# The first phase's shift columns and first scale column: made by TensorE from chunks with the condition's features on the partitions, instead of by VectorE and GpSimd

## The chip, the cores and the metric

One Trainium2 chip, of which the kernel uses one core. The metric is the time of one execution on the device, in microseconds. TensorE makes the matrix products and accumulates them in PSUM; VectorE, ScalarE and GpSimd work elementwise; SyncE issues the transfers (DMA) from the chip's memory to SBUF. Each engine takes its own instructions in the order in which the program gives them, and waits on semaphores for the others.

## The reference

A trunk of two layers on 512 positions of width 1024, in float32. Every sub-layer normalises its input and modulates it by a shift, a scale and a gate that come from one conditioning vector `c` (of 1024 features) through a matrix `ada_w`:

```python
c_act = jax.nn.silu(c)
for l in range(DEPTH):
    mod = (c_act @ ada_w[l] + ada_b[l]).reshape(b, N_MOD, 1, D_MODEL)
    sh1, sc1, g1 = mod[:, 0], mod[:, 1], mod[:, 2]
    ...
    h = modulate(rmsnorm(x, norm_ffn1[l]), sh1, sc1)      # h * (1 + sc1) + sh1
    x = x + 0.5 * g1 * swiglu(h, ffn1_wi[l], ffn1_wo[l])  # silu(h @ gate) * (h @ up) @ wo
    h = modulate(rmsnorm(x, norm_mix[l]), sh2, sc2)
    x = x + g2 * token_mixing(h, ...)
    h = modulate(rmsnorm(x, norm_ffn2[l]), sh3, sc3)
    x = x + 0.5 * g3 * swiglu(h, ffn2_wi[l], ffn2_wo[l])
return rmsnorm(x, final_norm)
```

This case is about `sh1` and `sc1` of the first layer: nothing of the first feed-forward can be multiplied before they are there.

## The kernel before

**Tiling.** Activations lie with their 1024 features in eight chunks of 128 partitions and the 512 positions in the free dimension. A modulation vector (shift, scale or gate) is therefore eight *columns*, 128x1 each, chunk k on the 128 partitions. Column (l, ch, k) of layer l is kept in `mod[:, l, ch, k]`; ch 0 is `sh1`, ch 1 is `sc1`. With its bias and, for a scale, the gain of the norm it goes to `fin`.

**Products in three parts.** Every float32 operand is split into `hi` (rounded to the fp32r type, ScalarE) and `lo` (the rest, VectorE); `mm3` (L224 to L228) makes hi x hi, lo x hi and hi x lo into one PSUM tile, each a 128x128 by 128x512 product.

**The first phase.** The first 60 us or so make the first five weight chunks (five PSUM tiles `ps`, in `start`) in eight steps k = 0 to 7, one for each chunk of features. A step is 15 products: three for each of the five chunks. It needs

- the chunk's slices of weights, loaded for two steps at once as 128x256 pieces (`raw`, L988), with `hi` (L989) and `lo` (L991);
- the normalised input of chunk k (`make`): `t` = x times scale column times the norm's factor (VectorE, L296), `hh` = t + shift column rounded (ScalarE, L298), `hl` = the rest (VectorE, L299);
- so the scale column and the shift column of chunk k, in `fin` (ScalarE, L983 and L984).

**How a column is made.** `ada_w` is stored transposed, so a transfer of 512 KB (`araw`, 128 outputs on the partitions, 1024 features along the row, L310) is multiplied by silu(c), copied to all partitions, and summed along the row. VectorE does both in one instruction (L320). For the shift columns of steps 1, 3, 4, 6 and 7 (`BY_POOL`) GpSimd multiplies (L317) and ScalarE sums in a pass over the product (L318). silu(c) is there twice, in SBUF (`cs`) and in PSUM (`pc`, two banks); in this phase VectorE reads the one in PSUM. Four `araw` buffers go round: the transfer for a column is issued when the column two steps back is done.

**Ahead of the first step.** TensorE copies c to all partitions (L363), runs small products on the identity matrix (`warm`, L942), sums the squares over the features (`pstat`, L273: a 128x128 block against one column of ones) and, when VectorE has the norm's factor, spreads it over the partitions (`pR`, L284).

**What sets the order.** A scheduler orders each engine's instructions by the order of the program, raised by `high_priority` and held back by `issue_after`. Behind the phase TensorE goes on with the remaining weight chunks of the same feed-forward, while VectorE makes the other modulation columns between its own work.

Of the kernel before, what the change touches and what calls it, by code (L numbers as in the profile page):

```python
# [11 lines left out]
F32 = mybir.dt.float32  # L12
F32R = mybir.dt.float32r
I32 = mybir.dt.int32
AF = mybir.ActivationFunctionType
ALU = mybir.AluOpType
PSUM = bass.MemoryType.PSUM

L = 2
KD = 8  # L20
S = 512
# [35 lines left out]
HL = 200  # L57
BY_POOL = (1, 3, 4, 6, 7)
AW = 1.5
# [8 lines left out]
@with_exitstack  # L68
def tile_trunk(ctx: ExitStack, tc: tile.TileContext, xT, c, positions, adaT, cols, sink, wi1, wo1,
               wqk, wv, w_out, wi2, wo2, masks, freqs, out):  # L70
    nc = tc.nc
    V, A, T, G = nc.vector, nc.scalar, nc.tensor, nc.gpsimd

    const = ctx.enter_context(tc.tile_pool(name="const", bufs=1))
# [6 lines left out]
    early = ctx.enter_context(ExitStack())  # L81
    pc = early.enter_context(tc.tile_pool(name="pc", bufs=1, space=PSUM)).tile([128, 1024], F32, name="pc")
    pq = None


    home = ctx.enter_context(tc.tile_pool(name="home", bufs=1))
    V.memset(home.tile([128, 56], F32, name="pad"), 0.0)

    x = const.tile([128, KD, S], F32, name="x")
    col = const.tile([128, cols.shape[1]], F32, name="col")  # L90
    ident = const.tile([128, 128], F32, name="ident")
    ones = const.tile([128, 1], F32, name="ones")
    orow = const.tile([1, 128], F32, name="orow")
    V.memset(ones, 1.0)
    V.memset(orow, 1.0)
    mod = const.tile([128, L, 9, KD], F32, name="mod")
# [4 lines left out]
    snk = const.tile([128, L * 8], F32, name="snk")  # L101
    nsnk = const.tile([128, L * 8], F32, name="nsnk")


# [201 lines left out]
    def ada_raw(l, ch, k):  # L306
        home, tags = ada["pool"]
        tags.append(tags.pop(0))
        raw = home.tile([128, 1024], F32, tag=tags[0], name="araw")
        nc.sync.dma_start(raw, adaT[l, ch * KD + k])  # L310
        return raw

    def ada_col(l, ch, k, pool=False, raw=None, by=cs):
        if raw is None:
            raw = ada_raw(l, ch, k)
        if pool:
            G.tensor_tensor(raw, raw, cs, op=ALU.mult)  # L317
            A.activation(raw, raw, AF.Copy, accum_out=mod[:, l, ch, k:k + 1])  # L318
            return
        return V.tensor_tensor_reduce(out=raw, in0=raw, in1=by, scale=1.0, scalar=0.0, op0=ALU.mult,  # L320
                               op1=ALU.add, accum_out=mod[:, l, ch, k:k + 1]).ins
# [36 lines left out]

    def ada_load(pool):
        cr = pool.tile([1, 1024], F32, tag="raw2", name="cr")  # L360
        nc.sync.dma_start(cr, c)
        for j in range(2):
            T.matmul(pc[:, j * S:(j + 1) * S], orow, cr[:, j * S:(j + 1) * S], start=True, stop=True)  # L363

    def ada_open(pool):
        ada["pool"] = pool, ["araw", "araw1", "araw2", "araw3"]
        for dst in (cs, pc):
            for j in range(2):
                A.activation(dst[:, j * S:(j + 1) * S], pc[:, j * S:(j + 1) * S], AF.Silu)

# [562 lines left out]
    with tc.high_priority():  # L933
        A.activation(snk[0:1, 0:1], orow[0:1, 0:1], AF.Silu)
    ada_load(pool)
    make_identity(nc, ident)
# [7 lines left out]
    norm = Norm()  # L944
# [5 lines left out]
    warm(WARM[0])  # L950
    with tc.issue_after(norm.last):
        ada_open(pool)
    nc.sync.dma_start(col, cols)
    cg = pool.tile([128, S], F32, tag="raw5", name="cg")[:, :KD]
    V.scalar_tensor_tensor(cg, col[:, KD:2 * KD], 1.0, col[:, C_NF1:C_NF1 + KD], op0=ALU.add, op1=ALU.mult)
    sc0 = ada_col(0, 1, 0, by=pc)
    with tc.high_priority():
        with tc.issue_after(sc0):
            norm.stat(0, 4)
        warm(WARM[1])  # L960
        norm.bcast(0, 4)
        warm(WARM[2])

    def start():
# [10 lines left out]
        norm.alloc()  # L975
        for k in range(KD):
            if k:
                with tc.issue_after(norm.first):
                    ada_col(0, 1, k, by=pc)
            with tc.issue_after(norm.first if k else norm.root):  # L980
                ada_col(0, 0, k, k in BY_POOL, by=pc)
            g = col[:, C_NF1 + k:C_NF1 + k + 1]
            A.activation(fin[:, 0, 1, k:k + 1], mod[:, 0, 1, k:k + 1], AF.Identity, scale=g, bias=cg[:, k:k + 1])  # L983
            A.activation(fin[:, 0, 0, k:k + 1], mod[:, 0, 0, k:k + 1], AF.Identity, bias=col[:, k:k + 1])  # L984
            if k % 2 == 0:
                ks = slice(k * 128, k * 128 + 256)
                for j, (raw, hi, lo) in enumerate(Ws):
                    nc.sync.dma_start(raw[:, ks], specs[j][:, ks])  # L988
                    A.activation(hi[:, ks], raw[:, ks], AF.Copy)  # L989
                    with nullcontext() if k else tc.issue_after(norm.root):  # L990
                        V.tensor_tensor(lo[:, ks], raw[:, ks], hi.bitcast(F32)[:, ks], op=ALU.subtract)  # L991
            with tc.high_priority():
                norm.make(k, 0, fin[:, 0, 1], fin[:, 0, 0], FULL)
            for (raw, hi, lo), p in zip(Ws, ps):
                mm3(p, (hi, lo), k, norm.h[k], FULL, k == 0, k == KD - 1)
# [183 lines left out]
```

## Time and profile before

| | us |
|---|---|
| median of 3 runs | 1952.32 (1952.02 to 1953.6) |
| the profiled execution | 1953.16 |
| its span, first to last instruction | 1951.4 |
| TensorE busy | 1907.5, 98% of the span |
| VectorE busy | 1514.6, 78% |
| ScalarE busy | 940.9, 48% |
| GpSimd busy | 84.7, 4% |

How to read the views: PE is TensorE's products, PEld its loads of weights, DVE is VectorE, ACT ScalarE, POOL GpSimd. PEclk is the share of full clock (2.4 GHz) that TensorE was granted in a stretch; 0.50 is its lower level, 1.2 GHz. In the windows each row is one stretch in us from the span's start, then its length, the busy time of each engine with its instructions, PEclk, the DMA share and GB/s. In the groups by line, behind the bar stand the busy us, the mean ns of one, and the idle us of the engine just before them with what ended them. In a timeline each row has start, us, engine, line, operation, out<-in, and in brackets the idle time before it. A float32 product of TensorE (`pstat`, `warm`, `pR`, `pc`) is shown as several passes with a weight load each; a product of `mm3` is one pass. The ends of passes are modelled and overlap the next start.

### The profile page before, as it was taken

The page shows a single profiled execution, that of the slowest core. Times are in us where ns is not written, and L with a number is a line of the kernel's source. Part 1 is how long each engine was busy: PE and PEld are TensorE (multiplying, and loading weights), DVE is VectorE, ACT ScalarE, POOL GpSimd, SP SyncE. Part 2 cuts the span into 40 slices and gives each one's busy share as a digit, 9 for nine tenths or more (in the row PEclk, how much of TensorE's full clock was granted, in tenths as well). Part 3 has the DMA queues.
Part 4 walks back from the last instruction along what each step waited for, and adds up shares of the span by engine and source line. Part 5 has one row for each costly group of instructions (what it writes and reads, how often), then busy time and mean ns, then how long its engine had stood idle before and what let it go on. Part 6 is the DMA issues. An engine that isn't in the chain of part 4 may idle for free.

```text
span 1951.4 us, 30979 instructions
## 1 busy us (share of the span) xinstructions
PE 1907.5 (98%) x12000; PEld 1714.8 (88%) x12000; DVE 1514.6 (78%) x2653; ACT 940.9 (48%) x1782; POOL 84.7 (4%) x63
## 2 busy tenths in 40 slices
PE   7999999999989999999999999999998999999998
PEld 5788888898777999989999898999887889898998
DVE  7967484477887989899688898867778889686773
ACT  5422222245674554536455363544566656353552
POOL 2000000021210000000000000000212000000000
PEclk8999999999999999999999999999999999999999
DMA  8878484244421246463424544342543113233231
GB/s 291 284 258 308 127 302 134 79 128 140 116 58 54 74 159 200 141 209 128 141 66 152 195 144 161 107 134 87 154 115 96 46 33 112 94 106 122 83 113 44
DMA packets 84677, 267.95 MB, mean 137 GB/s; under 512 B 10673, under 2 KB 13361, under 8 KB 84530
## 3 DMA queue, kind: packets, MB, share of 16 engines
q1 hardware_dynamic: 84530, 265.98, 42.4%
q8 instruction: 94, 1.54, 0.3%
q14 instruction: 53, 0.43, 0.1%
HBM read 244.97 MB, written 2.10 MB: 127 GB/s over the span
## 4 chain that ended last, share of the span: by engine, by line
PE 88%; DVE 5%; ACT 3%; issue 2%; DMA 2%; POOL 0%; SPq 0%; DVEq 0%; ACTq 0%; POOLq 0%
PE mm L226 17%; PE mm L227 17%; PE mm L228 16%; PE mm L488 10%; PE mm L489 9%; PE mm L490 9%; PE ptr L732 2%; PE po L739 1%; PE po L740 1%; PE s L698 1%; PE s L699 1%; DMA araw<-in_adaT_dram 1%; PE mm L661 1%; PE mm L662 1%; PE mm L663 1%
## 5 line engine op out<-in xcount | busy, mean ns | idle before, releaser
L157 ACT ACTIVATE hi<-raw 128x512 fp32r<-128x512 f32 (+5 forms) x253 | 215.2, 865 | 301.3 <-PE mm L228 213.7
L158 DVE TENSOR_TENSOR lo<-raw,hi 128x512 fp32r<-128x512 f32 (+5 forms) x253 | 258.6, 1033 | 85.4 <-ACT hi L157 84.3
L226 PE MATMUL mm<-hh,hi 128*128 128x512 f32 (+1 forms) x864 | 307.7, 357 | 6.9 <-ACT hh L298 6.6
L228 PE MATMUL mm<-hl,hi 128*128 128x512 f32 (+1 forms) x864 | 303.5, 355 | 3.1 <-DVE hl L299 3.1
L227 PE MATMUL mm<-hh,lo 128*128 128x512 f32 (+1 forms) x864 | 305.8, 355 | 0.0
L227 PE MATMUL mm<-gh,lo 128*128 128x512 f32 (+1 forms) x832 | 297.2, 357 | 0.0
L226 PE MATMUL mm<-gh,hi 128*128 128x512 f32 (+1 forms) x832 | 297.0, 357 | 0.0
L228 PE MATMUL mm<-gl,hi 128*128 128x512 f32 (+1 forms) x832 | 296.7, 357 | 0.0
L488 PE MATMUL mm<-sh,hi 128*128 128x256 f32 x912 | 260.2, 285 | 1.4 <-ACT sc L510 0.9
L489 PE MATMUL mm<-sh,lo 128*128 128x256 f32 x912 | 258.0, 283 | 0.0
L490 PE MATMUL mm<-sl,hi 128*128 128x256 f32 x912 | 258.0, 283 | 0.0
L185 ACT ACTIVATE hi<-raw 128x512 fp32r<-128x512 f32 x228 | 132.0, 623 | 140.3 <-issue 73.6
L396 DVE SCALAR_TENSOR_TENSOR x<-mm,fin,x 128x512 f32<-128x512 f32 (+1 forms) x156 | 101.9, 653 | 117.5 <-PE mm L228 116.8
L226 PEld LDWEIGHTS mm<-hh,hi 128*128 128x128 f32 x864 | 164.5, 191 | 29.6 <-ACT hh L298 8.1
L228 PEld LDWEIGHTS mm<-hl,hi 128*128 128x128 f32 x864 | 163.3, 190 | 26.1 <-DVE hl L299 4.9
L227 PEld LDWEIGHTS mm<-hh,lo 128*128 128x128 f32 x864 | 164.4, 190 | 20.9 <-DVE lo L991 0.6
L228 PEld LDWEIGHTS mm<-gl,hi 128*128 128x128 f32 x832 | 157.2, 189 | 22.7
L226 PEld LDWEIGHTS mm<-gh,hi 128*128 128x128 f32 x832 | 157.3, 189 | 22.2
L227 PEld LDWEIGHTS mm<-gh,lo 128*128 128x128 f32 x832 | 157.3, 189 | 22.2
L488 PEld LDWEIGHTS mm<-sh,hi 128*128 128x128 f32 x912 | 174.6, 191 | 2.1 <-ACT sc L510 1.1
L489 PEld LDWEIGHTS mm<-sh,lo 128*128 128x128 f32 x912 | 174.8, 192 | 0.0
L490 PEld LDWEIGHTS mm<-sl,hi 128*128 128x128 f32 x912 | 174.8, 192 | 0.0
(185 smaller groups left out, 4030.5 us busy)
## 6 DMA issues: line engine op xcount, KB each, us to landing
raw<-in_wi_dram SPq DMA_DIRECT2D x171, 512.0 KB, 3.8
araw<-in_adaT_dram SPq DMA_DIRECT2D x144, 512.0 KB, 4.7
raw<-in_wo_dram SPq DMA_DIRECT2D x64, 448.0 KB, 3.8
raw<-in_wo_dram SPq DMA_DIRECT2D x32, 512.0 KB, 3.6
raw<-in_wqk_dram SPq DMA_DIRECT2D x26, 512.0 KB, 3.7
raw<-in_w_out_dram SPq DMA_DIRECT2D x16, 512.0 KB, 3.8
kh<-qh SPq DMA_DIRECT2D x40, 128.0 KB, 2.3
kl<-t SPq DMA_DIRECT2D x40, 128.0 KB, 2.3
```

The source lines that it names most:

```text
L157: A.activation(hi[:, sl], raw[:, sl], AF.Copy)
L158: V.tensor_tensor(lo[:, sl], raw[:, sl], hi.bitcast(F32)[:, sl], op=ALU.subtract)
L185: A.activation(d, r, AF.Copy)
L226: T.matmul(ps, wh, X[0][:, s], start=start, stop=False)
L227: T.matmul(ps, wl, X[0][:, s], start=False, stop=False)
L228: T.matmul(ps, wh, X[1][:, s], start=False, stop=stop)
L396: ins = V.scalar_tensor_tensor(x[:, m, s], ps[:, s], gate[:, m:m + 1], x[:, m, s], op0=ALU.mult, op1=ALU.add).ins
L488: T.matmul(ps, wh, xh, start=start and k == 0, stop=False, skip_group_check=True)
L489: T.matmul(ps, wl, xh, start=False, stop=False, skip_group_check=True)
L490: T.matmul(ps, wh, xl, start=False, stop=stop and k == 3, skip_group_check=True)
L661: T.matmul(o, hh[:, ts], wh, start=k == 0, stop=False)
L732: T.transpose(p[:, j * 128:j * 128 + 128], self.sm[qt][:, c0:c0 + 128], ident)
```

## The change

`adaT` holds the nine chunks for `sh1` (all eight) and the first column of `sc1` in another layout: the condition's features on the partitions, so that a column is eight accumulated products of a 128x128 block with one column of silu(c) (`ct`, 128x8, a new input and a small transfer of its own). `pe_col` makes them on TensorE in PSUM; ScalarE's `fin` reads them there. The other seven scale columns stay on VectorE, reading `cs` in SBUF. GpSimd makes none; the copy of silu(c) in PSUM is gone, and its two banks are two buffers `pc` for the columns. silu(c) is made among the norm's squares, not behind them.

The columns of step k + 1 now stand in the program behind the first chunk's products of step k (`AT` = 1), where they stood at the head of their own step.

```diff
-BY_POOL = (1, 3, 4, 6, 7)
+AT = 1
...
-    pc = early.enter_context(tc.tile_pool(name="pc", bufs=1, space=PSUM)).tile([128, 1024], F32, name="pc")
+    pc = early.enter_context(tc.tile_pool(name="pc", bufs=2, space=PSUM))
...
+    def pe_col(l, ch, k):
+
+        raw = ada_raw(l, ch, k)
+        p = pc.tile([128, S], F32, tag="pc", name="pcol")[:, :1]
+        for j in range(KD):
+            T.matmul(p, raw[:, j * 128:j * 128 + 128], ct[:, j:j + 1], start=j == 0, stop=j == KD - 1)
+        return p
...
-        if pool:
-            G.tensor_tensor(raw, raw, cs, op=ALU.mult)
-            A.activation(raw, raw, AF.Copy, accum_out=mod[:, l, ch, k:k + 1])
-            return
...
     def ada_open(pool):
         ada["pool"] = pool, ["araw", "araw1", "araw2", "araw3"]
-        for dst in (cs, pc):
-            for j in range(2):
-                A.activation(dst[:, j * S:(j + 1) * S], pc[:, j * S:(j + 1) * S], AF.Silu)
+        cr = pool.tile([1, 1024], F32, tag="raw2", name="cr")
+        nc.sync.dma_start(ct, cT)
+        nc.sync.dma_start(cr, c)
+        A.activation(ct, ct, AF.Silu)
+        for j in range(2):
+            p = pc.tile([128, S], F32, tag="pc", name="pc")
+            T.matmul(p, orow, cr[:, j * S:(j + 1) * S], start=True, stop=True)
+            A.activation(cs[:, j * S:(j + 1) * S], p, AF.Silu)
...
-    with tc.issue_after(norm.last):
-        ada_open(pool)
...
-    sc0 = ada_col(0, 1, 0, by=pc)
     with tc.high_priority():
-        with tc.issue_after(sc0):
-            norm.stat(0, 4)
+        norm.stat(0, 4)
...
-        for k in range(KD):
+
+        def columns(k):
+
             if k:
                 with tc.issue_after(norm.first):
-                    ada_col(0, 1, k, by=pc)
-            with tc.issue_after(norm.first if k else norm.root):
-                ada_col(0, 0, k, k in BY_POOL, by=pc)
+                    ada_col(0, 1, k)
+                m = mod[:, 0, 1, k:k + 1]
+            else:
+                m = pe_col(0, 1, k)
             g = col[:, C_NF1 + k:C_NF1 + k + 1]
-            A.activation(fin[:, 0, 1, k:k + 1], mod[:, 0, 1, k:k + 1], AF.Identity, scale=g, bias=cg[:, k:k + 1])
-            A.activation(fin[:, 0, 0, k:k + 1], mod[:, 0, 0, k:k + 1], AF.Identity, bias=col[:, k:k + 1])
+            A.activation(fin[:, 0, 1, k:k + 1], m, AF.Identity, scale=g, bias=cg[:, k:k + 1])
+            A.activation(fin[:, 0, 0, k:k + 1], pe_col(0, 0, k), AF.Identity, bias=col[:, k:k + 1])
+
+        columns(0)
+        for k in range(KD):
...
-            for (raw, hi, lo), p in zip(Ws, ps):
+            for j, ((raw, hi, lo), p) in enumerate(zip(Ws, ps)):
+                if j == AT and k + 1 < KD:
+                    columns(k + 1)
                 mm3(p, (hi, lo), k, norm.h[k], FULL, k == 0, k == KD - 1)
...
+    for k in range(9):
+        adaT[0, k] = z["ada_w"][0, :, k * 128:k * 128 + 128].reshape(8, 128, 128).transpose(1, 0, 2).reshape(128, 1024)
```

**The order that results, TensorE ahead of step 0.** Before (`hh_216` is the input of step 0):

```order
L942 MATMUL warm<-ident 128x128 x17
L273 MATMUL pstat<-ones,acc 128x1 x4
L942 MATMUL warm<-ident 128x128
L284 MATMUL pR<-ident,ny 128x128 x4
L226 MATMUL mm<-hh_216,hi 128x512
```

With the change (`hh_215` is the input of step 0, `pcol` a column, the scale's first, then the shift's):

```order
L274 MATMUL pstat<-ones,acc 128x1 x4
L946 MATMUL warm<-ident 128x128 x2
L319 MATMUL pcol<-ct,araw 128x1 x8
L285 MATMUL pR<-ident,ny 128x128 x4
L319 MATMUL pcol<-ct,araw 128x1 x8
L227 MATMUL mm<-hh_215,hi 128x512
```

Two columns have come between the norm's sum and the first product.

**TensorE from step 0 to step 1.** Before (`hh0` is step 0's input, `hh1` step 1's):

```order
L226 MATMUL mm_215<-hh0_216,hi_209 128x512
L227 MATMUL mm_215<-hh0_216,lo_210 128x512
L228 MATMUL mm_215<-hl0_217,hi_209 128x512
L226 MATMUL mm_211<-hh1_218,hi_197 128x512
L227 MATMUL mm_211<-hh1_218,lo_198 128x512
```

With the change:

```order
L227 MATMUL mm_214<-hh0_215,hi_208 128x512
L228 MATMUL mm_214<-hh0_215,lo_209 128x512
L229 MATMUL mm_214<-hl0_216,hi_208 128x512
L319 MATMUL pcol_283<-ct_98,araw_281 128x1 x8
L227 MATMUL mm_210<-hh1_217,hi_196 128x512
L228 MATMUL mm_210<-hh1_217,lo_197 128x512
```

The shift column of step 1 stands directly ahead of step 1's products; so do those of steps 3, 5 and 7. The columns of steps 2, 4 and 6 stand behind the eighth product of the step before.

**ScalarE in step 1.** Before:

```order
L298 ACTIVATE hh_218<-t,fin 128x512
L989 ACTIVATE hi<-raw 128x256 x2
L983 ACTIVATE fin<-mod,cg,col 128x1
L989 ACTIVATE hi<-raw 128x256 x3
L984 ACTIVATE fin<-mod,col 128x1
L298 ACTIVATE hh_220<-t,fin 128x512
```

With the change (`fin<-pcol` reads the column that TensorE has made):

```order
L299 ACTIVATE hh_217<-t,fin 128x512
L986 ACTIVATE fin<-mod,cg,col 128x1
L987 ACTIVATE fin<-pcol,col 128x1
L995 ACTIVATE hi<-raw 128x256 x2
L299 ACTIVATE hh_219<-t,fin 128x512
```

Two `hi` now stand between the shift column of step 2 and its `hh`, the other three behind it.

## Rows read from the trace of the kernel before

**Rows 1.** Windows of the whole core: length, busy us of each engine, clock, DMA

```profile
16.70:26.80 10.10, 7.37 (x16) 5.13 (x17) 9.64 (x17) 5.08 (x13) 2.36 (x1) 0.50 0.69 221
...
26.90:60.00 33.10, 25.89 (x106) 19.11 (x106) 28.95 (x44) 18.40 (x42) 9.63 (x4) 1.00 0.87 304
...
59.80:100.00 40.20, 40.20 (x177) 33.32 (x178) 38.94 (x64) 15.80 (x21) 0.00 (x0) 1.00 0.79 283
...
50.70:57.60 6.90, 4.80 (x20) 3.66 (x21) 4.54 (x8) 3.62 (x8) 0.00 (x0) 1.00 0.91 316
...
614.10:620.70 6.60, 4.42 (x14) 3.60 (x15) 5.66 (x10) 2.28 (x5) 0.00 (x0) 0.50 0.26 79
...
1563.00:1569.60 6.60, 4.62 (x15) 3.76 (x16) 5.46 (x10) 2.33 (x4) 0.00 (x0) 0.50 0.23 79
```

**Rows 2.** Groups by line, 13 to 59 us: busy us, mean ns, idle before

```profile
L226 PE MATMUL mm<-hh,hi 128*128 128x512 f32 x40 | 17.5, 437 | 6.6 <-ACT hh L298 6.6
...
L320 DVE CUSTOM_DVE_ANT_0 araw<-araw,pc 128x1024 f32<-128x1024 f32 x11 | 13.3, 1215 | 0.9 <-ACT pc L369 0.9
...
L317 POOL TENSOR_TENSOR araw<-araw,cs 128x1024 f32<-128x1024 f32 x5 | 12.0, 2397 | 36.8 <-DMA araw<-in_adaT_dram 36.8
...
L991 DVE TENSOR_TENSOR lo<-raw,hi 128x256 fp32r<-128x256 f32 x20 | 11.9, 628 | 0.1
```

**Rows 3.** Timeline of TensorE in the first phase

```profile
12.37 1.05 PE L273 MATMUL pstat<-ones,acc 128*128 128x1 f32 x8 [0.49 <-DVE acc L267]
...
13.28 0.47 PE L942 MATMUL warm<-ident 128*128 128x128 f32 x2
...
18.89 0.80 PE L226 MATMUL mm<-hh,hi 128*128 128x512 f32 x1 [2.30 <-ACT hh L298]
...
24.04 0.63 PE L226 MATMUL mm<-hh,hi 128*128 128x512 f32 x1
...
24.46 0.63 PE L227 MATMUL mm<-hh,lo 128*128 128x512 f32 x1
...
55.78 0.50 PE L226 MATMUL mm<-hh,hi 128*128 128x512 f32 x1 [2.10 <-ACT hh L298]
...
59.10 0.39 PE L228 MATMUL mm<-hl,hi 128*128 128x512 f32 x1
...
59.78 0.50 PE L226 MATMUL mm<-hh,hi 128*128 128x512 f32 x1 [0.29 <-ACT sg L559]
```

**Rows 4.** Timeline of TensorE ahead of the stretch at half clock

```profile
610.75 0.40 PE L227 MATMUL mm<-yh,lo 128*128 128x512 f32 x1
...
610.99 1.04 PE L782 MATMUL pso<-ones,sqo 128*128 128x1 f32 x8
...
614.77 1.08 PE L790 MATMUL pRo<-ident,y 128*128 128x128 f32 x4 [1.71 <-DVE y L243]
```

**Rows 5.** Timeline of TensorE, two looks at one pstat of a later norm

```profile
994.58 0.17 PE L273 MATMUL pstat<-ones,acc 128*128 128x1 f32 x1
...
994.61 0.47 PE L273 MATMUL pstat<-ones,acc 128*128 128x1 f32 x3
```

**Rows 6.** Timelines: ScalarE in the first phase; one product and its reader

```profile
10.87 1.07 ACT L369 ACTIVATE cs<-pc 128x512 f32<-128x512 f32 x2
...
14.75 1.62 ACT L989 ACTIVATE hi<-raw 128x256 fp32r<-128x256 f32 x5
...
28.02 0.29 ACT L984 ACTIVATE fin<-mod,col 128x1 f32<-128x1 f32 x1 [1.03 <-DVE mod L320]
...
28.34 0.72 ACT L298 ACTIVATE hh<-t,fin 128x512 fp32r<-128x512 f32 x1
...
55.02 0.71 ACT L298 ACTIVATE hh<-t,fin 128x512 fp32r<-128x512 f32 x1
...
70.56 0.39 PE L228 MATMUL mm<-hl,hi 128*128 128x512 f32 x1
...
71.05 0.60 ACT L559 ACTIVATE sg<-mm 128x512 f32<-128x512 f32 x1 [0.96 <-PE mm L228]
```

More of the change, by code (lines that the diff above doesn't have):

```diff
@@ L68, in tile_trunk @@
 @with_exitstack
-def tile_trunk(ctx: ExitStack, tc: tile.TileContext, xT, c, positions, adaT, cols, sink, wi1, wo1,
+def tile_trunk(ctx: ExitStack, tc: tile.TileContext, xT, c, cT, positions, adaT, cols, sink, wi1, wo1,
                wqk, wv, w_out, wi2, wo2, masks, freqs, out):
@@ L81, in tile_trunk @@
     early = ctx.enter_context(ExitStack())
-    pc = early.enter_context(tc.tile_pool(name="pc", bufs=1, space=PSUM)).tile([128, 1024], F32, name="pc")
+    pc = early.enter_context(tc.tile_pool(name="pc", bufs=2, space=PSUM))
     pq = None
     home = ctx.enter_context(tc.tile_pool(name="home", bufs=1))
-    V.memset(home.tile([128, 56], F32, name="pad"), 0.0)
+    V.memset(home.tile([128, 48], F32, name="pad"), 0.0)
     x = const.tile([128, KD, S], F32, name="x")
@@ L102, in tile_trunk @@
     nsnk = const.tile([128, L * 8], F32, name="nsnk")
+    ct = const.tile([128, KD], F32, name="ct")
     def paired(l, sub, f):
@@ L311, in ada_raw, with ada_col @@
         return raw
-    def ada_col(l, ch, k, pool=False, raw=None, by=cs):
+    def pe_col(l, ch, k):
[4 more added lines that the diff above has]
+        return p
+    def ada_col(l, ch, k, raw=None):
         if raw is None:
             raw = ada_raw(l, ch, k)
-        if pool:
-            G.tensor_tensor(raw, raw, cs, op=ALU.mult)
-            A.activation(raw, raw, AF.Copy, accum_out=mod[:, l, ch, k:k + 1])
-            return
-        return V.tensor_tensor_reduce(out=raw, in0=raw, in1=by, scale=1.0, scalar=0.0, op0=ALU.mult,
+        return V.tensor_tensor_reduce(out=raw, in0=raw, in1=cs, scale=1.0, scalar=0.0, op0=ALU.mult,
                                op1=ALU.add, accum_out=mod[:, l, ch, k:k + 1]).ins
@@ L357, in ada_next @@
             ada_fin(l, ch)
-    def ada_load(pool):
-        cr = pool.tile([1, 1024], F32, tag="raw2", name="cr")
-        nc.sync.dma_start(cr, c)
-        for j in range(2):
-            T.matmul(pc[:, j * S:(j + 1) * S], orow, cr[:, j * S:(j + 1) * S], start=True, stop=True)
     def ada_open(pool):
         ada["pool"] = pool, ["araw", "araw1", "araw2", "araw3"]
-        for dst in (cs, pc):
-            for j in range(2):
-                A.activation(dst[:, j * S:(j + 1) * S], pc[:, j * S:(j + 1) * S], AF.Silu)
+        cr = pool.tile([1, 1024], F32, tag="raw2", name="cr")
[6 more added lines that the diff above has]
+            A.activation(cs[:, j * S:(j + 1) * S], p, AF.Silu)
     def group(norm, gs, sh, n):
@@ L934, in tile_trunk @@
         A.activation(snk[0:1, 0:1], orow[0:1, 0:1], AF.Silu)
-    ada_load(pool)
+    ada_open(pool)
     make_identity(nc, ident)
@@ L1149 @@
     w_out = z["w_out"].reshape(L, 2, 4, 128, 4, 2, 128).transpose(0, 1, 4, 3, 5, 2, 6).reshape(L, 2, 4, 128, 1024)
+    adaT = _np.ascontiguousarray(z["ada_w"].transpose(0, 2, 1)).reshape(L, 72, 128, 1024)
+    for k in range(9):
+        adaT[0, k] = z["ada_w"][0, :, k * 128:k * 128 + 128].reshape(8, 128, 128).transpose(1, 0, 2).reshape(128, 1024)
     arrays = {
@@ L1152 @@
         "c": z["c"].reshape(1, 1024),
+        "cT": z["c"].reshape(8, 128).T,
         "positions": z["positions"].reshape(1, 512),
-        "adaT": z["ada_w"].transpose(0, 2, 1).reshape(L, 72, 128, 1024),
+        "adaT": adaT,
         "cols": _np.concatenate(colparts, axis=1),
```

## The prediction

> **What bounds the kernel now.** I read three views, in this order. First the busy time by stretch [rows 1]: from 59.8 us on TensorE is busy in all of the stretch, so whatever moves the end of the first phase moves the end of the kernel by as much, unless TensorE is later given back time that it does not now lose. Before that it is not full: 7.37 of 10.10 us from 16.7 to 26.8, at half clock, and 25.89 of 33.10 us from 26.9 to 60.0, at full clock. VectorE, at 9.64 of 10.10 and 28.95 of 33.10, is the fuller one. So in the first phase VectorE sets the pace and TensorE waits. Second, the groups by line [rows 2] tell why: VectorE makes eleven column reductions of 1215 ns, and its `lo` subtractions average 628 ns, while five GpSimd multiplies of 2397 ns run in the same phase; and the first product of a step waits 6.6 us in all for ScalarE's `hh`. Third, TensorE in order of time [rows 3]: the first product starts at 18.89, the last of the phase at 59.10, the next phase's first at 59.78.
>
> **What goes.** Five GpSimd multiplies and their five ScalarE passes, four VectorE column reductions, and the two passes of Silu that put a second copy into PSUM. All of it is off TensorE. Its whole worth is TensorE's waits up to 59.8: at most 7.2 us at full clock (33.10 less 25.89), 2.7 us in the stretch at half clock, and what the clock itself costs there.
>
> **What comes.** Nine columns of eight products, 128x128 weights against one moving column. That form is in the trace: four products, eight passes, take from 12.37 to 13.28, 0.91 us [rows 3], so a column of sixteen passes holds TensorE for 1.82 us at full clock. Nothing hides this, since TensorE takes its products in order. Two columns stand ahead of the first step, seven among the steps: 7 x 1.82 = 12.7 us, more than the 9.9 us of waits that could be won. This is the term on which the sign hangs.
>
> The Trainium skill, page "TensorE: Matmul & The Clock Gate", section "LDWEIGHTS (loading the stationary operand)", has a load cost its columns over 1.2, 107 ns for 128. By that a column is an estimated 1.71 us, against 1.82 from the row; the sum would be about 1 us lower.
>
> **The new order adds waits.** The order shows the columns of steps 1, 3, 5 and 7 directly ahead of the step that needs them, with all of the step's products queued behind on TensorE. From a column's start S: its last pass starts at S + 1.71, lasts 0.25 (0.91 us hold eight that overlap; the row's busy time is 1.05), ScalarE starts 0.10 after a product's end (70.56 + 0.39 to 71.05 [rows 6]), so `fin` starts at S + 2.06; `hh` 0.32 later (28.02 to 28.34), the product 0.76 after that (55.02 to 55.78) [rows 3, 6]. That is S + 3.14: 1.82 of work and 1.32 of wait. For steps 2, 4 and 6 the column stands after eight of the previous step's fifteen products, with `fin`, two `hi` (0.31 each, five in 1.62 us [rows 6]) and `hh` in a row on ScalarE: S + 3.76, while TensorE works until S + 3.41; 0.35 of wait.
>
> **The sum at full clock.** A step of fifteen products takes 3.55 us (55.78 to 59.10, plus the last one's 0.23). An odd step starts 3.55 + 3.14 = 6.69 after the one before, an even one 1.96 (eight products) + 3.76 = 5.72. From step 0 to step 7: 4 x 6.69 + 3 x 5.72 = 43.9, and 3.55 for step 7: 47.5 us. Step 0 starts about 1.0 us later than 18.89. The two Silu passes (1.07 us [rows 6]) now stand among the squares instead of behind them and there is one DMA issue more ahead of `x`; of this I take 0.5 us, between nothing and 1.5. Then eight pstat passes, four of warm-up (0.45), the scale column (1.82), pR (0.44), the shift column, and `fin`, `hi`, `hh` in a row: 12.87 + 0.91 + 0.45 + 1.82 + 0.44 = 16.49, + 2.06 + 0.32 + 0.31 + 0.76 = 19.9. The phase ends at 19.9 + 47.5 = 67.4 instead of 59.33. The wait of 0.45 that stood behind it (59.33 to 59.78, for ScalarE's `sg`) is covered, since the first product of step 7 is done well before its end and ScalarE has little else: +8.1 - 0.45 = **+7.6 us**. VectorE (seven reductions of 1.2, 8.5 us, twenty `lo` and sixteen passes for `t` and `hl`, at most 12.6 and 13 us even at 0.63 and 0.8 each) fits within 43.9 us with room, and no load is late: each is issued when its buffer's column two steps back is done, 12.4 us ahead, and 512 KB at the 304 GB/s of the stretch [rows 1] take under 2. So TensorE and its chain through ScalarE are the new bound.
>
> **The clock.** At full clock is the doubtful half of that sentence. In the trace the clock is at half (1.2 GHz) from 614.1 to 620.7 [rows 1], after wide products, eight one-column passes (610.99), a few more wide products and a wait of 1.71 us [rows 4]; and again from 1563 to 1569.6, in the same place of the second layer [rows 1]. Between 50.7 and 57.6, where TensorE made wide products alone and waited as long as 2.10 us in one piece (ahead of 55.78), it stayed full [rows 1, 3]. So one-column passes seem not to hold the clock as wide ones do. In the changed phase every odd step is preceded by 1.82 us of just these and 1.32 us of nothing, and the start (pstat, column, pR, column, wait) has hardly a wide product from 12 to 20 us; before, with less still, it fell at 16.7. I therefore take it to fall: once at the start, as before, and about once in each of the three pairs of steps. A stretch at half lasts 6.6 to 10.1 us [rows 1]. At half a wide product takes 0.43 us (24.04 to 24.46 [rows 3]) instead of 0.23, so 47% of the stretch is lost: 3.1 to 4.7, say 4.0 each; four make 16, less about 1 for waits on ScalarE that don't grow. **+15 us**, between nothing and 37 (all eight steps, 120 x 0.20, and the seven columns at double, 12.7).
>
> **The forecast.** The profiled execution took 1953.16 us, 1.76 over its span and 0.84 over the median of the runs, 1952.32. On the median: 1952.3 + 7.6 + 15 = **1975 us**, 1.2% slower; on the profiled execution itself, 1976.
>
> **Rivals.** *The clock holds.* One-column passes might count, or the sequence at 614 fell for its wait alone; the fall at 1563, behind the same sequence, can't tell them apart. Against it stands the gap of 2.10 us at 53.7 that changed nothing. Then +7.6: 1960, still slower. Chance 0.22.
>
> *The weights are loaded ahead, and the kernel is not slower.* In one place the second of four one-column passes starts 0.03 us after the first (994.58, 994.61 [rows 5]), since a load had been made under the wide product before. If all sixteen came at 0.03, a column would be 0.48 us: `fin` at S + 0.80, an odd step at 3.55 + 1.88 = 5.43, an even one 1.96 + 2.50 = 4.46, step 0 at about 18.2, and the end 18.2 + 35.1 + 3.55 = 56.9: -2.4 - 0.45, so 1949.4. Low stretches are then short and the clock would hold. It decides at about 0.85 us a column. The same rows speak against it: the three passes from 994.61 last 0.47 us with 0.25 for one, so they start 0.11 apart, and the eight at 12.37 do too. The Trainium skill, same page, section "Wait — 56ns, not 53.3ns?", gives some 25 ns from start to start as the floor for small products; by that a column would be an estimated 0.40 us, and the trace shows 0.11 a pass instead. Chance 0.09, with what lies between.
>
> *Worse.* If nearly every step after the first were at half, 1985 and up to 1997 (the bound of 37). Chance 0.07. The forecast has the other 0.62, its own range 1963 to 1985.
>
> **Chances and range.** About 0.2%, 3.9 us, is what a measurement of this kernel can tell from no change. Slower takes the forecast, the worse case and nearly all of the clock that holds: 0.89. Same: 0.07, faster: 0.04, from the weights ahead. For 8 in 10 the range must reach over the case of the clock that holds, 1958 with step 0 not later, up to the end of the forecast's own: 1957.5 to 1985.
>
> **What the profile after would show.** GpSimd without any multiply in the phase and `lo` near 0.4 us each, if that part is right. Nine groups of sixteen one-column passes of 1.8 us each, longer where the clock is half; above 0.85 or below decides the sign. A wait of about 1.3 us for `hh` ahead of steps 1, 3, 5 and 7 and of 0.4 or less ahead of 2, 4 and 6. The granted clock at half in three or four stretches between 16 and 85 us; none of them after 30 us means that the second term is wrong. The last product of step 7 starting near 82 us (67 with the clock held). Past it TensorE as full as now; a new wait there would be a cost that I have not counted.

## The result, and the profile after

The changed kernel takes 1974.6 us (median of four runs, 1971.6 to 1975.9) against 1952.6 us: 1.011 times as long, 95% interval 1.0093 to 1.0128. The profiled execution took 1971.6 us, its span is 1969.8 us. The forecast was 1975 us.

The groups by line in the first phase, 12 to 73 us, answer to [rows 2] (columns as there):

```profile
L227 PE MATMUL mm<-hh,hi 128*128 128x512 f32 x40 | 20.1, 507 | 5.7 <-ACT hh L299 5.7
...
L319 PE MATMUL pcol<-ct,araw 128*128 128x1 f32 x144 | 16.9, 247 | 0.0
...
L325 DVE CUSTOM_DVE_ANT_0 araw<-araw,cs 128x1024 f32<-128x1024 f32 x7 | 8.5, 1221 | 0.0
L997 DVE TENSOR_TENSOR lo<-raw,hi 128x256 fp32r<-128x256 f32 x20 | 7.4, 420 | 10.2 <-ACT hi L995 10.2
```

GpSimd has no row any more, `lo` fell from 628 to 420 ns and waits for ScalarE instead of filling VectorE, and 144 one-column passes (nine columns of sixteen) have come to TensorE.

TensorE in order of time answers to [rows 3] (start us, us, instruction, in brackets the wait ahead of it and what ended it):

```profile
12.25 0.95 PE L274 MATMUL pstat<-ones,acc 128*128 128x1 f32 x8
...
13.59 1.84 PE L319 MATMUL pcol<-ct,araw 128*128 128x1 f32 x16
15.30 0.63 PE L285 MATMUL pR<-ident,ny 128*128 128x128 f32 x4
15.76 1.84 PE L319 MATMUL pcol<-ct,araw 128*128 128x1 f32 x16
18.87 0.80 PE L227 MATMUL mm<-hh,hi 128*128 128x512 f32 x1 [1.26 <-ACT hh L299]
...
25.03 1.84 PE L319 MATMUL pcol<-ct,araw 128*128 128x1 f32 x16
27.97 0.79 PE L227 MATMUL mm<-hh,hi 128*128 128x512 f32 x1 [1.10 <-ACT hh L299]
...
31.46 1.84 PE L319 MATMUL pcol<-ct,araw 128*128 128x1 f32 x16
33.16 0.48 PE L229 MATMUL mm<-hl,hi 128*128 128x512 f32 x1
...
34.88 0.50 PE L227 MATMUL mm<-hh,hi 128*128 128x512 f32 x1
...
38.44 1.84 PE L319 MATMUL pcol<-ct,araw 128*128 128x1 f32 x16
41.39 0.65 PE L227 MATMUL mm<-hh,hi 128*128 128x512 f32 x1 [1.10 <-ACT hh L299]
...
73.17 0.39 PE L229 MATMUL mm<-hl,hi 128*128 128x512 f32 x1
73.40 0.39 PE L227 MATMUL mm<-hh,hi 128*128 128x512 f32 x1
```

A column holds TensorE for 1.70 us (31.46 to 33.16) and its last pass ends at 1.84. Steps 0, 1 and 3 stand here behind a column and a wait for `hh`; so do 5 and 7. Step 2 (34.88) follows a column made in the middle of step 1 and waits for nothing. The next phase begins at 73.40 instead of 59.78 [rows 3]: **13.6 us** later, with no wait ahead of it.

The windows answer to [rows 1] (stretch, length, busy us of PE, PEld, DVE, ACT, POOL, then the granted clock, DMA share, GB/s):

```profile
17.70:24.50 6.80, 5.63 (x13) 4.51 (x14) 4.41 (x9) 2.74 (x8) 0.00 (x0) 0.50 0.81 257
24.50:27.90 3.40, 2.37 (x19) 2.13 (x17) 0.00 (x0) 0.96 (x2) 0.00 (x0) 1.00 0.15 42
27.90:31.30 3.40, 3.33 (x8) 2.65 (x9) 2.64 (x4) 0.41 (x2) 0.00 (x0) 0.50 0.51 166
...
41.60:45.00 3.40, 3.40 (x10) 2.66 (x9) 2.41 (x4) 0.39 (x1) 0.00 (x0) 0.50 0.54 188
55.20:58.60 3.40, 3.40 (x11) 2.75 (x10) 2.27 (x4) 0.39 (x1) 0.00 (x0) 0.50 0.99 383
68.90:72.30 3.40, 3.40 (x10) 2.63 (x9) 2.41 (x5) 2.35 (x5) 0.00 (x0) 0.50 0.29 111
72.40:100.00 27.60, 27.60 (x124) 22.83 (x123) 25.55 (x42) 9.24 (x13) 0.00 (x0) 1.00 0.76 287
```

The clock is at half five times in the phase, 20.4 us in all: once at the start, and then each time just as step 1, 3, 5 or 7 begins, behind its column and its wait. From 72.4 us TensorE is full. So 13.6 us were lost in the phase, and the span is 18.4 us longer than before (1969.8 against 1951.4): some 5 us went where the program is the same as before. The experiments are about these two.

### The profile page after: what moved, and what is told of

It reads as the page before. It is cut to its first block, busy times and chain, and to the rows that moved or that the text cites. A ratio compares the mean times of both kernels' runs of the same rounds, so it can differ in the third digit from the quotient of the medians.

```text
span 1969.8 us, 31257 instructions
## 1 busy us (share of the span) xinstructions
PE 1933.8 (98%) x12144; PEld 1730.9 (88%) x12144; DVE 1504.5 (76%) x2645; ACT 934.8 (47%) x1771; POOL 72.4 (4%) x58
## 4 chain that ended last, share of the span: by engine, by line
PE 92%; DVE 4%; ACT 2%; issue 1%; DMA 1%; SPq 0%; POOL 0%; DVEq 0%; ACTq 0%
PE mm L227 18%; PE mm L228 17%; PE mm L229 17%; PE mm L492 10%; PE mm L493 10%; PE mm L494 10%; PE ptr L736 2%; PE po L743 1%; PE po L744 1%; PE s L702 1%; PE mm L665 1%; PE mm L667 1%; PE mm L666 1%; PE s L703 1%; PE pcol L319 1%
```

## The experiments

Each kernel's time is the median of its runs; before, beside them on the same chips, had 1952.3 to 1953.1. "Next phase" is the start of the first product behind the phase in the profile, 59.78 before.

| kernel | columns on TensorE | addresses | us | next phase |
|---|---|---|---|---|
| before | none | before | 1952.7 | 59.78 |
| after | 9 of one-column passes, 4 ahead of their step | moved | 1974.6 | 73.40 |
| x3_ct_home | the same | before | 1967.4 | 73.43 |
| x1_narrow_mid | 9 of one-column passes, those of the steps all in mid-step | moved | 1966.2 | |
| x5_narrow_mid_home | the same | before | 1959.5 | 69.25 |
| x2_wide_same | 9 of 128-column passes, 4 ahead of their step | moved | 1963.0 | 67.88 |
| x10_wide_same_home | the same | before | 1961.4 | 68.17 |
| x6_wide_mid_home | 9 of 128-column passes, those of the steps all in mid-step | before | 1955.1 | 62.67 |
| x7_no_gpsimd | none, and none on GpSimd | before | 1947.1 | 55.81 |
| x8_mix3 | 4 of 128-column passes | before | 1945.7 | 54.57 |
| x11_mix4 | 5 of 128-column passes | before | 1947.4 | 58.40 |
| x4_before_moved | none (before) | moved | 1957.8 | 59.16 |
| x9_both_moved | none (before) | all moved | 1955.4 | 58.96 |

### Where the buffers lie: x3, x4, x9

Behind the first phase the two programs make the same products, yet the changed one fell back further. The change adds one tile of 32 bytes, `ct`, to the pool `const`, and cuts the pad in `home` by as much. The pools lie in the order in which they are opened, so those between the two (the weights `hi` and `lo`, and `hh`, `hl`) lie 32 bytes further on, and those behind the pad (with `gh`, `gl`, `sh`, `sl`) where they were. x3 puts `ct` beside the pad, and x4 does the move alone, in the kernel before:

```diff
 # x3_ct_home, against after
     V.memset(home.tile([128, 48], F32, name="pad"), 0.0)
+    ct = home.tile([128, KD], F32, name="ct")
...
-    ct = const.tile([128, KD], F32, name="ct")
 # x4_before_moved, against before
-    V.memset(home.tile([128, 56], F32, name="pad"), 0.0)
+    V.memset(home.tile([128, 48], F32, name="pad"), 0.0)
...
+    V.memset(const.tile([128, KD], F32, name="ct"), 0.0)
```

> The changed kernel with its one new tile, ct (32 bytes in each partition), allocated in another pool, so that every other buffer in SBUF has the address that it has in the kernel before. The instructions and their order are the same. Theory C (the about 5 us that the changed kernel lost after its first phase come from where its buffers lie: 512-column products at 0.231 to 0.235 us in many tiles instead of 0.227): they come back, 1974.6 - 5 = 1970 us, and the offset against the kernel before stays near 13.6 us from 120 us to the end. Theory D (they come from the clock or from the heat of the chip): 1974.6 us, with the same drift from 13.6 to about 18.4 us.

> The kernel before with one unused tile of 32 bytes put where the changed kernel has ct, and the pad cut by as much: every buffer has the address that it has in the changed kernel, and the first phase is that of before (one VectorE memset of eight columns more). Theory C (the addresses cost about 5 us after the first phase): 1952.6 + 5 = 1957.6 us, with a drift against the kernel before that grows from nothing at 60 us to 5 at the end. Theory D: 1952.6 us.

x3 took 1967.4 us (1963.7 to 1969.2), 7.2 less than after, with the same first phase to 0.03 us. x4 took 1957.8 us, ratio 1.0024 (1.0015 to 1.0033), 5.1 more than before. Both came out as theory C has it, x3 by 2.2 us more than its 5. The mean granted clock of x3's runs is 0.987 against 0.985 for after, so part of the 7.2 can be the clock; x4's is 0.989, as that of before beside it, and its 5.1 is the cleaner size.

The traces show the drift without the clock, which stays full between the two products of this table in all five profiles:

| kernel | first product of the next phase | first `pstat` of the next norm | between |
|---|---|---|---|
| before | 59.78 | 383.31 | 323.53 |
| after | 73.40 | 399.57 | 326.17 |
| x3_ct_home | 73.43 | 396.84 | 323.41 |
| x4_before_moved | 59.16 | 385.33 | 326.17 |
| x9_both_moved (below) | 58.96 | 382.39 | 323.43 |

With the weights moved the same work takes 2.6 us longer, in after and in x4 alike. The groups by line with shapes kept apart, over the whole span, show which products it is; of x4:

```profile
L489 PE MATMUL mm<-sh,hi 128*128 128x256 f32 x912 | 258.7, 284 | 0.3 <-ACT sc L519 0.2
...
L227 PE MATMUL mm<-gh,hi 128*128 128x512 f32 x576 | 227.8, 395 | 0.0
```

and of x3, where all lies as before:

```profile
L492 PE MATMUL mm<-sh,hi 128*128 128x256 f32 x912 | 260.0, 285 | 0.0
...
L227 PE MATMUL mm<-gh,hi 128*128 128x512 f32 x576 | 224.2, 389 | 0.0
```

The 512-column products on `gh` and `gl`, 3 x 576, take 389 ns each where the buffers lie as before and 395 or 396 where the weights have moved: 3 x 3.6 = 10.8 us. The 256-column ones on `sh` and `sl` gain 1 to 2 ns, 4.7 us in all, and other 256-column products gain a little too. What is left is best read from the starts: x4 begins the next phase 0.6 us ahead of before, and its span is 3.5 us longer (1954.8 against 1951.4), so 4.1 us are lost behind the phase. The profile after has the same row as x4:

```profile
L227 PE MATMUL mm<-gh,hi 128*128 128x512 f32 x576 | 227.8, 395 | 0.0
```

In x4 weights had moved and `gh` had not. x9 leaves the pad at 56, so that both move:

```diff
 # x9_both_moved, against x4
-    V.memset(home.tile([128, 48], F32, name="pad"), 0.0)
+    V.memset(home.tile([128, 56], F32, name="pad"), 0.0)
```

> The kernel before with the same unused tile of 32 bytes as x4_before_moved (1957.8 us), but with the pad left whole: now the buffers behind the pad (the pools of the phases, which hold the activations gh, gl and sh) move by 32 bytes together with those ahead of it (the weights hi and lo, and hh and hl), where in x4 only those ahead moved. Theory E (what counts is where a product's moving operand lies as against its weights): nothing has moved against each other, 1952.8 us, and the products of gh are spaced as in the kernel before. Theory F (what counts is each buffer's own address): the weights are where they are in x4, so 1957.8 us or another time that is not that of before.

```profile
L227 PE MATMUL mm<-gh,hi 128*128 128x512 f32 x576 | 224.2, 389 | 0.0
```

The products are back at 389 ns: at this shift of 32 bytes, what counts is where a product's moving operand lies as against its weights (theory E), not either address. So does the stretch in the table above, 323.43 us. The time bears it out in part: 1955.4 us, ratio 1.001 (1.0001 to 1.0019), less than x4's by 2.4 and more than before by 3.1. The mean clock of x9's median run is 0.987 against 0.990 for before beside it. Over all runs x9 has 0.9887 and 1954.6 us on average, before 0.9898 and 1952.6; 0.11% of 1950 us is an estimated 2.1 us, so the clock is enough to account for the difference. That it does was not tried, and why it would have fallen more often stays open.

### The clock: x1, x2, x5, x10

Two things stand ahead of each of the four later falls in the changed kernel: a column of one-column passes, and a wait of 1.1 us. One kernel takes the wait away from behind the column, by making every column after the ninth product of the step ahead (x1; x5 with the addresses of before). The other keeps the columns of steps 1, 3, 5 and 7 and their waits where they are and makes each pass 128 columns wide, all copies of the same (x2; x10 with the addresses of before).

```diff
 # x1_narrow_mid, against after (x5 has the two lines of x3 besides)
-                if j == AT and k + 1 < KD:
-                    columns(k + 1)
                 mm3(p, (hi, lo), k, norm.h[k], FULL, k == 0, k == KD - 1)
+                if k + 1 < KD and j == 2:
+                    with tc.issue_after(state["third"]):
+                        shift = pe_col(0, 0, k + 1)
+                    columns(k + 1, shift)
 # x2_wide_same, against after (x10 has the two lines of x3 besides)
-        p = pc.tile([128, S], F32, tag="pc", name="pcol")[:, :1]
+        p = pc.tile([128, S], F32, tag="pc", name="pcol")[:, :128]
...
-            T.matmul(p, raw[:, j * 128:j * 128 + 128], ct[:, j:j + 1], start=j == 0, stop=j == KD - 1)
+            T.matmul(p, raw[:, j * 128:j * 128 + 128], ct[:, j:j + 1].to_broadcast([128, 128]), ...)
```

In x1 `state["third"]` is the ninth product of the step, and the products behind it are held back until the column is issued. x2 and x10 differ from after in more than the width: the columns of steps 2, 4 and 6 are held behind the ninth product as well (the eighth in after), and the code of a column stands later in the program, so that ScalarE takes all five `hi` of step 2 ahead of its shift column, where in after they came behind it. The four columns ahead of their step stand where they did.

> The changed kernel with every shift column made after nine products of the step ahead of it, the columns of steps 1, 3, 5 and 7 too, which stand in the changed kernel directly ahead of their step, with a wait of 1.1 us for hh behind them. Nothing else differs. Theory A (the one-column passes let the clock fall, the wait does not): the four waits of about 1.0 to 1.1 us go, the granted clock still falls in the phase, about as often as in the changed kernel (five stretches of 3.4 to 6.8 us): 1974.6 - 4 = 1970.6 us. Theory B (the waits let it fall): the waits go and with them the four falls after 25 us, which cost 47% of 3.41 us each: 1974.6 - 4 - 6.4 = 1964 us, and no stretch at half between 26 and 80 us.

> The changed kernel with each column pass made over 128 moving columns that all read the same feature column, so that it writes 128 equal columns of which one is used; the columns stand where they do in the changed kernel, four of them directly ahead of their step. Theory A (one-column passes let the clock fall): the falls after 25 us go, the waits of 1.1 us stay: 1974.6 - 6.4 = 1968 us, less up to 3 more if the stretch at the start shortens too, and up to 2 more back if a column of wide passes is 0.2 us longer. Theory B (the waits let it fall): the four falls stay where they are, 1974.6 us and no stretch less.

> Every shift column in the middle of the step ahead, of one-column passes, and all buffers at the addresses that they have in the kernel before: this is the kernel x1_narrow_mid with the allocation of x3_ct_home, so that its profile can be laid beside that of x3 (1967.4 us). Theory A (one-column passes alone let the clock fall): the four stretches at half between 26 and 73 us stay, only the waits of 1.1 us go: 1967.4 - 4 = 1963.4 us. Theory B (the wait behind them is needed): at most one stretch at half is left after 26 us: 1967.4 - 4 - 5 = 1958 us.

x1 took 1966.2 us (median of five; a disturbed execution of nearly twice the time, the profiled one, is left out, so no row of x1 stands here), between its theories. x2 took 1963.0 us (1962.7 to 1963.9), 11.7 less than after. Windows of x2:

```profile
16.70:26.70 10.00, 7.79 (x52) 6.80 (x51) 5.98 (x12) 3.98 (x11) 0.00 (x0) 1.00 0.58 177
26.70:72.00 45.30, 40.38 (x219) 33.66 (x220) 32.66 (x57) 19.60 (x43) 0.00 (x0) 1.00 0.86 307
```

The clock stays full from 16.7 to 72 us, the start included, though the waits are still there (timeline of TensorE, x10, the same at the addresses of before):

```profile
23.35 1.94 PE L319 MATMUL pcol<-ct,araw 128*128 128x128 f32 x16
...
26.40 0.50 PE L227 MATMUL mm<-hh,hi 128*128 128x512 f32 x1 [1.11 <-ACT hh L299]
...
68.17 0.50 PE L227 MATMUL mm<-hh,hi 128*128 128x512 f32 x1 [1.22 <-ACT sg L563]
```

That is what theory A expects, so a wait of this length alone is not the cause. Nor is a wide column shorter: it holds TensorE for 1.70 us as well (28.59 to 30.29 in x10). But x5, one-column passes with no wait behind them, took 1959.5 us (1956.8 to 1963.6), 7.9 less than x3 and near theory B. Its windows:

```profile
18.60:32.20 13.60, 12.96 (x38) 10.84 (x39) 7.82 (x16) 4.68 (x13) 0.00 (x0) 0.50 0.49 165
32.30:73.00 40.70, 38.06 (x211) 31.50 (x210) 24.46 (x44) 15.08 (x35) 0.00 (x0) 1.00 0.65 229
```

Behind 32.3 us the clock stays full over six columns of one-column passes. x5 is not free of waits: ahead of steps 3, 5 and 7 it still has 0.65, 0.67 and 0.78 us, but six wide products stand between the column and each of them:

```profile
60.90 1.84 PE L319 MATMUL pcol<-ct,araw 128*128 128x1 f32 x16
...
65.02 0.50 PE L227 MATMUL mm<-hh,hi 128*128 128x512 f32 x1 [0.78 <-ACT hh L299]
```

So neither theory holds alone: with wide passes the waits of 1.1 to 1.7 us did nothing, and one-column passes with wide products behind them did nothing once the clock was up; where the wait stood directly behind the column it fell, four times of four, in after and again in x3. A column and its wait are together 2.8 us without a wide product. Longer waits alone were followed by falls too (see the end), so these runs don't tell whether the column adds something of its own or only makes the gap between wide products longer. What x5 has besides is a longer stretch at half at the start, 13.6 us against 6.8 in x3; the first two columns and a wait of 1.26 us stand ahead of it, and the column of step 1 in it. So in this one profile half of the 13.6 us at half that were saved later were paid at the start, and its phase ends only 4.2 us before x3's.

x10 was the fourth corner:

> Columns of 128-column passes, four of them directly ahead of their step as in the changed kernel, all buffers at the addresses of the kernel before. It fills the fourth corner of a table whose others are one-column passes ahead of the step (x3, 1967.4 us), one-column passes in the middle (x5, 1959.5) and 128-column passes in the middle (x6, 1955.1). If the clock falls only where one-column passes and a wait of 1.1 us stand together, the clock stays full here and against x6 only the four waits come: 1955.1 + 4 x 0.9 = 1958.7 us. Rival: wide passes are cheaper for another reason than the clock, and the step from x3 is the 4.4 us of x5 to x6: 1963 us.

It took 1961.4 us (1958.7 to 1962.4), between its theories, so the times alone decide nothing. The phases of the four corners, at the addresses of before, read: 73.43 (one column, ahead), 69.25 (one column, mid), 68.17 (128, ahead), 62.67 (128, mid). Width is worth 5.3 us ahead of the step and 6.6 in the middle; place 4.2 and 5.5. Place costs more than four waits of 1.1: x10's are 1.1 to 1.7 us (the longest stands behind a `hi` that waited for its transfer), and the 1.22 for `sg` comes on top. Width in the middle is mostly the clock at the start: x5's 13.6 us at half cost an estimated 47% of that, 6.4 us, and x6 has none.

### GpSimd's half alone, and the blend: x7, x6, x8, x11

x7 is the kernel before with the five GpSimd columns on VectorE; x6 has all nine columns on TensorE in the best form of the above (wide, mid-step, addresses of before).

```diff
 # x7_no_gpsimd, against before
-BY_POOL = (1, 3, 4, 6, 7)
+BY_POOL = ()
 # x8_mix3, against x6: TensorE makes the first scale column and the shift columns 0, 3 and 6
+BY_PE = (0, 3, 6)
...
+            if k in BY_PE:
+                m = shift if k else pe_col(0, 0, k)
+            else:
+                with tc.issue_after(norm.first):
+                    ada_col(0, 0, k)
+                m = mod[:, 0, 0, k:k + 1]
 # x11_mix4, against x8
-BY_PE = (0, 3, 6)
+BY_PE = (0, 1, 3, 5)
```

> The kernel before with the five GpSimd columns given to VectorE, and TensorE making none: the first half of the change alone, without what it adds on TensorE. Theory (GpSimd's multiplies held VectorE up): lo from 628 to 420 ns, twenty times, and hl from 1107 to 751, eight times, give back 7.0 us of VectorE against five reductions of 1.3 us that come, 6.5 us: 1952.7 - 0.5 = 1952 us, the phase ends within 1 us of 59.33. Rival (lo and hl are slow for another reason, as the clock or the transfers): 1952.7 + 6.5 = 1959 us.

x7 took 1947.1 us (1944.4 to 1949.0), ratio 0.9968 (0.9956 to 0.9981): faster than before by 5.9 us, more than its theory had. Its phase ends 4.0 us earlier. Groups by line from 12 to 59 us and one window:

```profile
L320 DVE CUSTOM_DVE_ANT_0 araw<-araw,pc 128x1024 f32<-128x1024 f32 x16 | 19.1, 1214 | 1.0 <-ACT pc L369 1.0
...
L991 DVE TENSOR_TENSOR lo<-raw,hi 128x256 fp32r<-128x256 f32 x20 | 7.5, 418 | 0.0
...
16.70:60.00 43.30, 36.76 (x139) 28.07 (x139) 41.65 (x77) 20.49 (x46) 0.00 (x0) 0.89 0.90 299
```

Five reductions have come to VectorE, but `lo` takes 418 ns instead of 628 [rows 2] beside no GpSimd, as in after. The Trainium skill, page "GPSIMD Engine Reference", section "8. Key points", has GpSimd share its SBUF interfaces with VectorE, with contention for VectorE's instructions with two SBUF inputs; the rows agree, 210 ns on each such `lo`. What the expectation left out is that VectorE also idles less: 41.65 of 43.30 us busy against 38.59 of 43.20 before [rows 1], some 3 us. GpSimd's five columns and their passes are gone from ScalarE's queue; that this is the reason was not tried. The 1.9 us beyond the phase are not in this profile, which ends 4.2 us before that of before; x7's runs have a mean clock of 0.992 against 0.989.

> Columns of 128-column passes (x2_wide_same, 1963 us), every one in the middle of the step ahead, and all buffers at the addresses that they have in the kernel before. If the three causes add up (the clock, the four waits of about 1.1 us, the addresses 7 us): 1963 - 4.4 - 7.2 = 1951.5 us, no stretch at half in the first 100 us and no wait for hh above 0.5 us behind step 0. Rival: with the waits gone ScalarE or VectorE is late next, the steps with a column stay 0.5 us or more apart from their 5.4 us: 1955 us.

x6 took 1955.1 us (1953.3 to 1957.6), the rival's time; two waits for `hh` of 0.5 us or more are left, one of 1.10 ahead of step 0 and this of 0.79 ahead of step 5, and one for `sg` behind the phase:

```profile
47.60 0.50 PE L227 MATMUL mm<-hh,hi 128*128 128x512 f32 x1 [0.79 <-ACT hh L299]
...
62.67 0.50 PE L227 MATMUL mm<-hh,hi 128*128 128x512 f32 x1 [0.54 <-ACT sg L563]
```

Against x7 it is 8.0 us slower, 6.9 of it in the phase: what the columns on TensorE cost at full clock and at the addresses of before, against a kernel whose own phase had 10.2 us at half clock (15.9 to 22.7 and 43.2 to 46.6). Seven columns of 1.70 us in the steps are 11.9, less the waits that they fill.

> A blend: TensorE makes the first scale column and the shift columns 0, 3 and 6, in 128-column passes, those of 3 and 6 in the middle of the step ahead; VectorE makes the other five shift columns besides its seven scale columns; GpSimd makes none; all buffers at the addresses of the kernel before. On TensorE the phase then needs 28.4 us of products and two columns of 1.8 within the steps, from 18.9 on: 51.5 us at the earliest. On VectorE twelve reductions of 1.3 us, twenty lo of 0.42, sixteen passes of 0.75: 36 us from about 16, 52 us with nothing in between and 56 with the waits that the changed kernel shows. End at 52 to 57 instead of 59.33: 1946 to 1950 us, say 1948. Rival: the shift columns on VectorE come as late as in the kernel before, TensorE waits for them as it did there: 1952 us.

x8 took 1945.7 us (1944.9 to 1946.3), ratio 0.9961 (0.9948 to 0.9975), 2.3 below its forecast and just under the range; it beats both kernels, by 7.4 us the one before, by 29 the changed one. TensorE and VectorE in its phase:

```profile
16.70:54.50 37.80, 33.95 (x164) 26.55 (x163) 33.69 (x63) 19.59 (x48) 0.00 (x0) 1.00 0.93 327
...
41.65 0.50 PE L227 MATMUL mm<-hh,hi 128*128 128x512 f32 x1 [1.32 <-ACT hh L299]
```

Both engines are near 34 of 37.8 us, at full clock. From x7 it is 1.4 us, and the ranges of the two overlap, so most of the gain is the half without TensorE, and whether the rest is one stays open.

> The blend x8_mix3 (1945.7 us) with the shift columns 0, 1, 3 and 5 on TensorE instead of 0, 3 and 6: the waits that TensorE had in x8 stood ahead of the steps 1 (0.84 us), 2 (0.35) and 5 (1.32), whose shift columns, or the one before, VectorE made. Theory (VectorE is late there): one reduction less on VectorE, 1.3 us, and a column more on TensorE, 1.7 us, against waits of about 2 us: 1945 us, between 1943.5 and 1946. Rival (the waits move to the steps 2, 4 and 6): 1947.4 us, the column's 1.7 on top.

x11 took 1947.4 us (1944.6 to 1948.8), the rival's time, by another way: the waits ahead of steps 1, 2 and 5 went, and one of 3.26 us came ahead of step 7. ScalarE's timeline shows it taking the next phase's `hi` first, which waited for a transfer; `fin` and `hh` of step 7 stood behind it:

```profile
51.28 0.63 ACT L158 ACTIVATE hi<-raw 128x512 fp32r<-128x512 f32 x1 [2.19 <-DMA raw<-in_wi_dram]
51.82 0.28 ACT L993 ACTIVATE fin<-mod,col 128x1 f32<-128x1 f32 x1
52.00 0.61 ACT L158 ACTIVATE hi<-raw 128x512 fp32r<-128x512 f32 x1
52.52 0.71 ACT L299 ACTIVATE hh<-t,fin 128x512 fp32r<-128x512 f32 x1
```

## Why the prediction was right, point by point

The sign and the way there were right: columns that nothing hides, waits behind them, and a clock that falls. That the total came out to 0.4 us was luck: the clock's term was too large by some 9 us, and 8 us came from behind the phase, where the sum had nothing.

**Signs that came as said.** GpSimd makes nothing in the phase and `lo` is at 420 ns. The nine columns take 1.70 us, against 1.82 in the sum; the passes start 0.11 us apart, so the rival with weights loaded ahead (0.48 us a column, deciding at 0.85) is out. Columns of steps 1, 3, 5 and 7 stand directly ahead, behind each a wait of 1.10 (1.32 in the sum); from a column's start to the product it is 2.94 us (25.03 to 27.97; 3.14 in the sum). The even steps wait for nothing; the sum had 0.35 us. The next phase follows without a wait, as said.

**The term at full clock, +7.6 us,** is the best of it. x2 and x10 are the changed phase with the clock held: 67.88 and 68.17 against 59.78, +8.1 and +8.4. In x10 step 0 begins at 19.81 (19.9 in the sum) and the last product of step 7 starts at 66.57, so that the steps end at 66.8 (67.4 in the sum). Only the wait of 0.45 us that the sum let go is not gone at full clock: it is 1.22 us for `sg` in x2 and x10, where ScalarE makes it later than TensorE is done with step 7. In the changed kernel itself step 0 was not later than before, 18.87 against 18.89: `pstat` started at 12.25 there (12.87 in the sum), the first column is 0.1 us shorter, and from the second column's start to the product it is 3.11 us (3.45 in the sum).

**The clock, +15 us, is the step that was mis-sized.** Its mechanism holds, and its count nearly: one fall at the start, and behind it four, one at each odd step, against three in the sum. But the four last 3.4 us each and not the 6.6 to 10.1 that the sum took from [rows 1]. The trace of before had a stretch of that length too, which the prediction did not look at:

```profile
562.80:566.20 3.40, 3.40 (x16) 2.90 (x14) 2.05 (x5) 1.57 (x4) 0.94 (x1) 0.50 0.48 154
```

Measured by after against x2 the clock costs 73.40 - 67.88 = 5.5 us, or 6.8 from the first product of step 0 on (54.5 us against 47.8), since x2 began that step at 20.12; x2's other differences are in either figure. The phase is thus 13.6 us longer and not 22.6. Its reason was also only half right: "one-column passes seem not to hold the clock as wide ones do" was seen where a wait followed them directly; in x5, with wide products behind them, they did not drop it.

**What the sum did not have** is the third term, 5 us for the addresses (x4: +5.1 by medians; x3: 7.2). The kernel's full edit has it, as a tile added in one pool and a pad cut in another; it was taken for nothing. With 13.6 and 5.1 the medians' 22.0 leave some 3 us. In the profiled execution one fall behind the phase is longer than its like in before:

```profile
577.50:587.70 10.20, 8.10 (x30) 7.10 (x31) 7.18 (x20) 5.26 (x14) 1.27 (x1) 0.50 0.37 104
```

The fall there lasted 3.4 us before (562.8 to 566.2). It costs little: the changed kernel is 16.8 us behind at the same product ahead of it (546.04 against 529.20) and 18.1 behind it (624.08 against 605.99). The profiled execution is also the fastest of the four, 18.4 us behind by its span, so most of the 3 us lie in runs without a profile. Such falls differ in length from run to run; the mean clock of the changed kernel's runs is 0.984 to 0.987, but the runs of 1971.6 and 1975.25 us both have 0.985. What the 3 us are stays open.

**The rivals.** That the clock holds is what x2 makes true by other means: 1963 us with the addresses moved, 1961 without, where the prediction gave 1960. The worse case (1985) did not come. On the engine that sets the pace the prediction was right too: VectorE idles in the changed phase (10.2 us ahead of `lo` alone), TensorE with its chain through ScalarE is the bound.

## What to carry to other kernels

Take the two halves of such a change apart: what it frees (GpSimd, 5.9 us here) and where it puts the work. On an engine that takes its instructions in order, a column of small passes costs its full 1.7 us, a wait behind it costs again, and the two together can take the clock as well; the same column in the middle of a step, in passes as wide as 128, cost no clock and, but for 0.79 us at one step, no wait (x6). A new tile, however small, is part of the change: look which pools it moves against which.

## What the runs showed of the hardware that was not expected

- **Products depend on where their operands lie against each other.** 32 bytes between the weights' pool and that of `gh` made 1728 products 6 to 7 ns longer (389 to 395 or 396) and 2736 others 1 to 2 ns shorter, 2.6 us in the first 320 behind the phase; with both moved (x9) the 389 came back.
- **One-column passes with a wait of 1.1 us directly behind them were followed by a fall, and neither was where it stood apart from the other.** 1.70 us of the one and 1.1 us of the other were followed by a fall four times of four in after and in x3; 128-column passes in their place, with waits of 1.1 to 1.7 us, never were, and the clock stayed up even at the start, where in every profile but those with wide columns it fell between 15.9 and 18.6 us.
- **A longer wait alone was followed by a fall too, but not always.** The prediction took the gap of 2.10 us ahead of 55.78 [rows 1, 3], where the clock stayed full, as evidence that waits don't matter. In x7 one of 2.19 ahead of 42.42, in x4 one of 2.10 ahead of 54.03, in x9 one of 2.60 ahead of 53.82 and in x11, with wide columns, one of 3.26 ahead of 53.28 were followed by a fall:

```profile
43.20:46.60 3.40, 3.40 (x9) 2.65 (x8) 3.31 (x8) 1.69 (x5) 0.00 (x0) 0.50 1.00 392
...
55.00:58.40 3.40, 3.40 (x9) 2.65 (x9) 1.57 (x2) 2.66 (x4) 0.00 (x0) 0.50 0.54 210
...
55.20:58.60 3.40, 3.40 (x10) 2.65 (x9) 2.23 (x2) 2.98 (x4) 0.00 (x0) 0.50 0.40 157
...
53.50:57.00 3.50, 3.50 (x9) 2.75 (x9) 0.80 (x2) 1.38 (x2) 0.00 (x0) 0.51 0.55 224
```

So one gap that changed nothing, in one profile, was no proof for the next.
